# An encoder layer in float32: w_o by seven block products with the sums in DRAM, and every up-projection unit by seven products

## The chip, the cores and the metric

The kernel runs on one core of one Trainium2 chip. A core has TensorE (PE in the profile; matrix products into eight PSUM banks), VectorE (DVE), ScalarE (ACT), GpSimd (POOL) and SyncE (SP). Each takes its own instructions in order. DMAs are issued from the queues of SP, ACT and POOL. The metric is the device time of one execution in microseconds (us).

## The reference

One layer of a hybrid encoder on 512 tokens of width 2048, all in float32:

```python
h = rms_norm(x, pre_mix_g[l])
z = h @ w_in[l]                                  # q | k | v | u, 1024 columns each
a = chunked_attention(q, k, v, rel_bias[l])      # 8 heads of 128
p = multiscale_pool(u, pool_w[l], pool_scale[l])
m = jnp.concatenate([a, p], axis=-1) @ w_o[l]    # (512, 2048) @ (2048, 2048)
x = x + rms_norm(m, post_mix_g[l])
h = rms_norm(x, pre_ffn_g[l])
up = causal_dwconv(h @ w_up[l], conv_w[l], conv_b[l])   # 2 x 5632 columns, 3 taps
y = (gelu(up[..., :D_FF]) * up[..., D_FF:]) @ w_down[l] # (512, 5632) @ (5632, 2048)
x = x + rms_norm(y, post_ffn_g[l])
```

The gains, the relative bias, the pooling scale and the convolution's bias are random; the output is (1, 512, 2048).

## The kernel before, in words

Every large product is made three times on rounded parts. `split` (L127) writes a value's rounded part (`hi`, ScalarE, L129 or L132) and the rest (`lo`, VectorE, L130 or L133); `mm3` (L144) adds hi x hi, lo x hi and hi x lo into one PSUM bank. A tile that `mm3` reads therefore costs one ScalarE and one VectorE pass.

`Weights` (L55) hands out weight tiles of 128 x 1024 numbers (512 KB): `load_w` (L137) loads one on SP's queue into a raw tile (5 in the ring) and splits it into a ring of 8 (four pairs), four tiles ahead of use.

The stages follow each other on TensorE. Its order is the program's (L85); the instructions of the other engines and the DMA issues are put in order by a planner, which issues what is ready.

- **Projections.** h of the first norm stands with features on partitions (`hT`). q and k of head 0 are made while x arrives; then v of four heads, q and k per head, scores, softmax, values (L324, L349, L361), and eight projections u with pooling (`pool_keep`, L372). `mixT` holds the heads, `mT` the split concatenation.
- **w_o, features on partitions** (L464 to L528). 16 blocks of 128 output features; each is 16 x 3 matmuls whose stationary tile is w_o and whose moving tile is mT, 512 tokens wide. The result waits in `mg`, times the gain; squares are added up over features on POOL (L499).
- **The seam** (L531 to L599). Token sums by matmuls with ones (L160), a power on POOL for the reciprocal root mean square, 64 transposes that turn m back to tokens on partitions (L536) and store it in DRAM (`mtokd`), a spread of the token factors (L170), and `x2` (L568): multiply, add x, split into the second h (`gT`), square and add.
- **Up projection.** A unit u has 256 gate and 256 value columns. The first PLAIN = 3 units are whole products (L587 to L596, `up` L746). h goes in without the second norm's factor; the result is multiplied by it (`normed` L740, `keep_all` L917). The other 19 units, as 38 blocks k, use Strassen's scheme in Winograd's form: a block (128 x 2 columns, 512 tokens, 2048 features) is cut in two along all three, and seven products of half size (`seven` L928: 8 x 3 matmuls, 256 tokens wide) are combined afterwards (`keep_six` L902, `keep_all`). The weight sums for the products are made by adding DMAs from POOL into raw tiles (`add` L859) and one addition on VectorE (L866); the token factors, sums of quarters of h, are made once (`h_sums` L794). `Factors` (L822) orders the products and keeps four split ahead.
- **The rest of a unit.** Three taps (`taps` L708), gelu, product, and a store to DRAM (`gd`). `residual` (L934) makes x + norm(m) for the output rows beside blocks 4 to 20.
- **Down projection.** Five chunks of 1024 rows, also by seven products (`multiply` L681), summed in DRAM by adding DMAs (`keep_product` L688); the last two units plainly (`last`, L1127).

Memory is taken from pools that open and close; a tile in a pool that opens later waits for the tiles that lay there.

Of the kernel before, what the change touches and what calls it, by code (L numbers as in the profile page):

```python
# [30 lines left out]
PLAIN = 3  # L31
CU = 4
AHEAD = 3
SCALE = 1.0 / math.sqrt(DH)
# [41 lines left out]
def encoder_layer(ctx: ExitStack, tc: tile.TileContext, x, xT, vecs, rel, post_ffn,  # L76
# [15 lines left out]
    psum = ctx.enter_context(tc.tile_pool(name="psum", bufs=8, space=bass.MemoryType.PSUM))  # L92
    dram = ctx.enter_context(tc.tile_pool(name="dram", bufs=1, space=bass.MemoryType.DRAM))

    def bank(name):
        return psum.tile([P, 512], F32, tag="ps", name=name)
# [4 lines left out]
    def raw4(name):  # L101
        return big.tile([P, 1024], F32, tag="raw", bufs=5, name=name)
# [46 lines left out]
    def new_hT(name):  # L149

        return [[big.tile([P, 4, S], F32R, tag="hT", bufs=8, name=f"{name}{part}{i}") for i in range(4)]
                for part in "hl"]

    def blk(hT, kb, sl=slice(None)):
        return tuple(hT[part][kb // 4][:, kb % 4, sl] for part in range(2))
# [42 lines left out]
    for g in range(4):  # L198
        for j in range(2):
            specs += halves(f"u{2 * g + j}", w_in, head_cols("u", 2 * g + j), 8, P)  # L200
        if g:
            specs += pm_spec(g - 1)
    for n in range(8):
        s = halves(f"wo{n}", w_o, n * 256, 4, 256)
        specs += s[:-1] + pm_spec(3) + s[-1:] if n == 0 else s
    for u in range(PLAIN):
        gate, up_ = ([(f"w{p}{u}_{i}", w_up[u, p, :, i // 2, :, i % 2 * 512:(i % 2 + 1) * 512].rearrange(
            "m p c -> p m c"), 2, 512) for i in range(4)] for p in range(2))
        specs += [s for pair in zip(gate, up_) for s in pair] if u == 0 else gate + up_
# [4 lines left out]
    RR = const.tile([P, 2, S], F32, name="RR")  # L214
    R = RR[:, 0, :]
    rt = const.tile([P, NT], F32, name="rt")
    xt = [acc8(f"xT{i}", "AABB"[i]).rearrange("p (a b) -> p a b", a=4) for i in range(4)]
    hT = new_hT("hT")
# [21 lines left out]
    nc.sync.dma_start(vec[:, V_CONV:], vecs[:, V_CONV:])  # L240

# [6 lines left out]
    with tc.tile_pool(name="p1", bufs=2, reuse_waits="tile") as p1:  # L248
# [24 lines left out]
        zero = t512("u", bufs=2)[:, :P]  # L273
# [121 lines left out]
        def pool_mix(g, keep_):  # L395
            w = weights.get(f"pm{g}")
            d = [state.pop(("pool", g, a)) for a in range(2)]
            for j in range(2):
                ps = bank(f"pm{g}_{j}")
# [42 lines left out]
        mixT.append(acc8("mixT2", "B").rearrange("p (a b) -> p a b", a=4))  # L442
# [5 lines left out]
        u7 = project("u7")  # L448


        mT = new_hT("mT")

        def keep_mT(kb, ps, scale):
            split(*blk(mT, kb), ps, scale)

        for kb in range(4):
            split(*blk(mT, kb), mix(kb))
        pool_mix(2, keep_mT)
        for kb in range(4, 8):
            split(*blk(mT, kb), mix(kb))  # L460
        pool_keep(3, 1, u7)
        for kb in range(8, 12):
            split(*blk(mT, kb), mix(kb))
        wo0 = [bank(f"m{j}") for j in range(2)]  # L464

        def wo_block(ps, w, kb, j):
            mm3(ps, part(w, kb % 4, slice(j * P, (j + 1) * P)), blk(mT, kb), kb == 0, kb == KD - 1)

        for i in range(3):
            w = weights.get(f"wo0_{i}")  # L470
            for kb in range(4 * i, 4 * i + 4):
                for j in range(2):
                    wo_block(wo0[j], w, kb, j)
        pool_mix(3, keep_mT)
        w = weights.get("wo0_3")
        for kb in range(12, 16):
            for j in range(2):
                wo_block(wo0[j], w, kb, j)

    mg = [acc8(f"mg{i}", "AABB"[i]).rearrange("p (a b) -> p a b", a=4) for i in range(4)]  # L480
    rm = const.tile([P, NT], F32, name="rm")
    mtokd = [dram.tile([P, D], F32, name=f"mtokd{t}") for t in range(NT)]
    x2d = [dram.tile([P, D], F32, name=f"x2d{t}") for t in range(2, NT)]

    with tc.tile_pool(name="p2", bufs=2, reuse_waits="tile") as p2:
        ssum = p2.tile([P, S], F32, name="ssum", bufs=1)

        def wo_keep(cb, ps):
            sq = p2.tile([P, S], F32, tag="sq", bufs=2, name="sq")
            nc.scalar.activation(sq, ps, AF.Square)  # L490
            nc.scalar.activation(mg[cb // 4][:, cb % 4, :], ps, AF.Copy, scale=col(V_POSTMIX, cb))
            return sq

        sqs = []

        def wo_add(cb, ps):
            sqs.append(wo_keep(cb, ps))
            if cb:
                nc.gpsimd.tensor_add(ssum, sqs[-1], sqs[0] if cb == 1 else ssum)  # L499

        for j in range(2):
            wo_add(j, wo0[j])
        for n in range(1, 7):
            ps = [bank(f"m{2 * n + j}") for j in range(2)]
            for i in range(4):
                w = weights.get(f"wo{n}_{i}", 0 if n == 6 and i else None)
                for kb in range(4 * i, 4 * i + 4):
                    for j in range(2):
                        wo_block(ps[j], w, kb, j)
            for j in range(2):  # L510
                wo_add(2 * n + j, ps[j])
        xc = []

        def load_xc(kb):
            c = p2.tile([P, S], F32, tag="xc", bufs=5, name=f"xc{kb}")
            nc.scalar.dma_start(c, xT[kb * P:(kb + 1) * P, :])
            xc.append(c)

        ws = [weights.get(f"wo7_{i}", 3 - i) for i in range(4)]
        for kb in range(5):  # L520
            load_xc(kb)
        for j in range(2):
            ps = bank(f"m{14 + j}")
            for kb in range(KD):
                wo_block(ps, ws[kb // 4], kb, j)
            if j == 0:
                wo_add(14, ps)
        last = wo_keep(15, ps)  # L528
        weights.prefetch(2)

        mtok = [p2.tile([P, D], F32, name=f"mtok{t}", bufs=1) for t in range(NT)]  # L531

        def turn_back(t, g):
            ps = bank(f"mt{t}_{g}")
            for i in range(4):
                nc.tensor.transpose(ps[:, i * P:(i + 1) * P], mg[g][:, i, t * P:(t + 1) * P], ident)  # L536
            return t, g, ps

        def turned(t, g, ps, engine):
            dest = mtok[t][:, g * 512:(g + 1) * 512]  # L540
            if engine:
                nc.vector.tensor_copy(dest, ps)
            else:
                nc.scalar.activation(dest, ps, AF.Copy)
            nc.sync.dma_start(mtokd[t][:, g * 512:(g + 1) * 512], dest)

        psr = bank("Rm")
        token_sums(psr[:, NT:], ssum)
        before = p2.tile([P, NT], F32, name="before", bufs=1)
        nc.vector.tensor_scalar(before, psr[:, NT:2 * NT], 1.0 / D, EPS, op0=ALU.mult, op1=ALU.add)  # L550
        for t in range(2):
            turned(*turn_back(0, t), t)
        token_sums(psr, last)
        nc.vector.scalar_tensor_tensor(rm, psr[:, :NT], 1.0 / D, before, op0=ALU.mult, op1=ALU.add)
        nc.gpsimd.tensor_tensor(rm, rm, mhalf, op=ALU.pow)
        weights.prefetch(4)
        rest = [(0, 2)] + [(t, g) for t in range(1, 3) for g in range(3)]
        for i, (t, g) in enumerate(rest):
            turned(*turn_back(t, g), i % 2)
        spread(psr, rm)  # L560
        later = [(3, g) for g in range(3)] + [(t, 3) for t in range(NT)]
        pending = [turn_back(*p) for p in later[:3]]


        hT = new_hT("gT")
        ss2 = p2.tile([P, S], F32, name="ss2", bufs=1)

        def x2(kb):  # L568
            v = mg[kb // 4][:, kb % 4, :]
            nc.vector.tensor_mul(v, v, psr)  # L570
            (nc.gpsimd if kb % 2 else nc.vector).tensor_add(v, v, xc[kb])
            split(*blk(hT, kb), v, col(V_PREFFN, kb))
            sq = p2.tile([P, S], F32, tag="sq", bufs=2, name="sq2")
            nc.scalar.activation(sq, v, AF.Square)
            sqs.append(sq)
            if kb:
                nc.gpsimd.tensor_add(ss2, sq, sqs[-2] if kb == 1 else ss2)
# [22 lines left out]

    mixing.close()

# [154 lines left out]

# [460 lines left out]
```

## Time and profile before

| | |
|---|---|
| median of 3 runs | 1961.03 us (1959.75 to 1962.8) |
| profiled execution: its span, first to last instruction | 1954.2 us |
| what lies around the span, against the median | 6.8 us |
| TensorE busy | 1929.5 us |
| VectorE, ScalarE, POOL busy | 1405.5, 890.2, 311.7 us |
| w_o, first to last matmul | 405.6 to 582.5 us |
| seam, up to the first up-projection matmul | 582.5 to 591.9 us |
| plain units | 591.9 to 731.4 us |
| units by seven products | 731.4 to 1496.7 us |
| DMA | 335.51 MB, mean 172 GB/s |

The profile is of one execution. Each row of a group gives the line, the engine, the operation, what it writes and reads with shapes, the count, the busy time and the mean of one in ns, and the idle time before with what ended it. A matmul's listed length is longer than the distance between two, since they overlap.

### The profile page before, as it was taken

How to read it: one execution, taken by the hardware profiler on the slowest of the kernel's cores; microseconds unless marked ns; L12 is line 12 of the kernel's file. 1: busy time of each engine (PE TensorE's matmuls, PEld its weight loads, DVE VectorE, ACT ScalarE, POOL GpSimd, SP SyncE). 2: the span in 40 equal slices, each digit the busy share in tenths (PEclk: the TensorE clock that was granted, in tenths of full speed). 3: DMA queues.
4: the chain of work that ended last, by engine and by line, in shares of the span. 5: the costliest groups of instructions: out<-in, count | busy, mean ns of one | idle time of the engine just before them, and what ended most of it. 6: DMA issues, size and time to landing. Idle time of an engine off the chain costs nothing.

```text
span 1954.2 us, 28600 instructions
## 1 busy us (share of the span) xinstructions
PE 1929.5 (99%) x11594; PEld 1721.6 (88%) x11594; DVE 1405.5 (72%) x1573; ACT 890.2 (46%) x1092; POOL 311.7 (16%) x377
## 2 busy tenths in 40 slices
PE   9999999999999999999999999999999899999998
PEld 7888888888887889999999999999998688888886
DVE  5554255562229867787888878788888999998877
ACT  6333233242236434444454445444445555465443
POOL 4000000001117001111111211111110121221221
PEclk9999999999999999999999999999999999999999
DMA  7433332332235356768887887767675789999997
GB/s 241 116 89 92 92 92 70 98 127 96 97 97 198 119 160 152 163 161 220 214 212 198 201 225 183 188 150 184 167 183 179 264 213 263 246 222 231 214 223 228
DMA packets 176499, 335.51 MB, mean 172 GB/s; under 512 B 10480, under 2 KB 78448, under 8 KB 175088
## 3 DMA queue, kind: packets, MB, share of 16 engines
q1 hardware_dynamic: 135824, 219.39, 33.6%
q0 software_dynamic: 38240, 110.12, 29.9%
q10 hardware_dynamic: 2304, 4.20, 0.7%
q8 instruction: 90, 1.47, 0.3%
q14 instruction: 41, 0.34, 0.0%
HBM read 272.84 MB, written 60.82 MB: 171 GB/s over the span
## 4 chain that ended last, share of the span: by engine, by line
PE 92%; DVE 4%; DMA 2%; issue 1%; ACT 0%; SPq 0%; POOL 0%; ACTq 0%; POOLq 0%; DVEq 0%
PE q L146 15%; PE q L147 14%; PE q L145 14%; PE p L145 6%; PE p L147 6%; PE p L146 6%; PE m L147 3%; PE m L145 3%; PE m L146 3%; PE up L146 2%; PE up L147 2%; PE up L145 2%; PE u L145 1%; PE u L146 1%; PE v L146 1%; PE v L145 1%
## 5 line engine op out<-in xcount | busy, mean ns | idle before, releaser
L146 PE MATMUL q<-gTl,wfh 128*128 128x256 f32 x1216 | 344.0, 283 | 0.0
L147 PE MATMUL q<-gTh,wfl 128*128 128x256 f32 x1216 | 343.9, 283 | 0.0
L145 PE MATMUL q<-gTh,wfh 128*128 128x256 f32 x1216 | 343.8, 283 | 0.0
L145 PEld LDWEIGHTS q<-gTh,wfh 128*128 128x128 f32 x1216 | 233.1, 192 | 0.0
L147 PEld LDWEIGHTS q<-gTh,wfl 128*128 128x128 f32 x1216 | 233.1, 192 | 0.0
L146 PEld LDWEIGHTS q<-gTl,wfh 128*128 128x128 f32 x1216 | 232.9, 192 | 0.0
L146 PE MATMUL p<-bl,ah 128*128 128x512 f32 x560 | 221.2, 395 | 4.7 <-DVE bl L130 4.7
L145 PE MATMUL p<-bh,ah 128*128 128x512 f32 x560 | 222.4, 397 | 2.8 <-ACT ah L129 2.8
L147 PE MATMUL p<-bh,al 128*128 128x512 f32 x560 | 221.8, 396 | 2.3 <-DVE al L130 2.3
L129 ACT ACTIVATE wfh<-wx 128x1024 fp32r<-128x1024 f32 x152 | 158.8, 1056 | 120.5 <-PE q L146 80.3
L130 DVE TENSOR_TENSOR wfl<-wx,wfh 128x1024 fp32r<-128x1024 f32 x152 | 183.9, 1220 | 35.6 <-ACT wfh L129 35.5
L130 DVE TENSOR_TENSOR bl<-b,bh 128x2048 fp32r<-128x2048 f32 x70 | 159.2, 2285 | 14.2 <-PE p L146 8.4
L129 ACT ACTIVATE bh<-b 128x2048 fp32r<-128x2048 f32 x70 | 133.0, 1913 | 68.7 <-DVE b L660 52.6
L146 PEld LDWEIGHTS p<-bl,ah 128*128 128x128 f32 x560 | 105.7, 189 | 30.1 <-DVE bl L130 5.4
L129 ACT ACTIVATE wfh<-wy 128x1024 fp32r<-128x1024 f32 x76 | 80.6, 1060 | 113.3 <-PE q L146 72.7
L147 PEld LDWEIGHTS p<-bh,al 128*128 128x128 f32 x560 | 105.9, 189 | 29.0 <-DVE al L130 3.7
L145 PEld LDWEIGHTS p<-bh,ah 128*128 128x128 f32 x560 | 105.7, 189 | 27.8 <-ACT ah L129 3.7
L860 POOL DMA_DIRECT2D wx<-in_w_up x76 | 67.5, 889 | 381.8 <-DVE wfl L130 366.3
L702 POOL DMA_DIRECT2D sum<-part x60 | 72.5, 1235 | 256.1 <-DVE part L693 120.3
L130 DVE TENSOR_TENSOR wfl<-wy,wfh 128x1024 fp32r<-128x1024 f32 x76 | 92.7, 1220 | 26.8 <-ACT wfh L129 26.3
L146 PE MATMUL q<-h4l,wfh 128*128 128x256 f32 x304 | 86.0, 283 | 0.0
L146 PE MATMUL q<-h7l,wfh 128*128 128x256 f32 x304 | 86.0, 283 | 0.0
(430 smaller groups left out, 4844.3 us busy)
## 6 DMA issues: line engine op xcount, KB each, us to landing
b<-in_w_down SPq DMA_DIRECT2D x42, 1024.0 KB, 7.8
wx<-in_w_up POOLq DMA_DIRECT2D x76, 512.0 KB, 6.7
sum<-part POOLq DMA_DIRECT2D x70, 512.0 KB, 7.8
wx<-in_w_up SPq DMA_DIRECT2D x40, 512.0 KB, 5.7
wy<-in_w_up SPq DMA_DIRECT2D x38, 512.0 KB, 5.4
wz<-in_w_up SPq DMA_DIRECT2D x38, 512.0 KB, 6.1
wy<-in_w_up POOLq DMA_DIRECT2D x38, 512.0 KB, 7.1
gd<-ca POOLq DMA_DIRECT2D x40, 256.0 KB, 3.3
```

Of the source, the lines that this page charges most:

```text
L129: rounded = nc.scalar.activation(hi, src, AF.Copy)
L130: nc.vector.tensor_sub(lo, src, f32(hi))
L145: nc.tensor.matmul(ps, l[0], r[0], start=first, stop=False)
L146: nc.tensor.matmul(ps, l[0], r[1], start=False, stop=False)
L147: nc.tensor.matmul(ps, l[1], r[0], start=False, stop=last)
L702: nc.gpsimd.dma_start(dest, v, accum_op=ALU.add)
L860: nc.gpsimd.dma_start(self.raw[k, what], self.block(k, m, kh), accum_op=ALU.add)
```

## The change

w_o is computed by the same seven-product scheme, now with tokens on partitions: the stationary tile is a 128-token piece of a factor made from the mixed heads, the moving tile is 512 columns of a factor made from w_o. Four of the seven w_o factors are sums of quarters of w_o; they are formed in DRAM (`wo_sum`) by plain copies on SP's queue and adding DMAs on POOL's, 32 steps of 1 MB, one of which is written before each projection (`next(summing)`) and before every second tile of v. Each product of 1024 x 256 tokens x 1024 columns takes 4 bank groups (`wo_product`); `mixed` adds the products up on VectorE, takes squares along the row on ScalarE and multiplies by the gain.

With tokens on partitions the norm is a factor per partition: `norms` makes x + norm(m), stores it, takes the second norm and scales; `turned` transposes the normed x (64 transposes) and writes it with the second gain as h. Tokens 0 to 255 are done during the last two products, tokens 256 to 511 after them.

The up projection takes this normed h, so the multiplication by the spread factor disappears. All 22 units (44 blocks) go by seven products. For the first EARLY = 4 blocks the products that need only tokens 0 to 255 (1 and 2) come first, with the transposes of the other tokens between them; then the other five for blocks 0 and 1, then for 2 and 3, with all their weight sums by adding DMAs. The token factors are combined from h in between (`combine`). Signs of the odd columns are taken into the convolution weights. PSUM banks are named by hand. The residual step, `mtokd`, the token sums and the spread are gone.

```diff
-PLAIN = 3
+EARLY = 4
@@
-        return big.tile([P, 1024], F32, tag="raw", bufs=5, name=name)
+        return big.tile([P, 1024], F32, tag="raw", bufs=6, name=name)
@@
+    WO_ORDER = 1, 2, 6, 7, 4, 5, 3
+    for n in WO_ORDER:
+        for cc in range(2):
+            s = [(f"wo{n}{cc}_{q}", rows(wo_factor[n], q * 256, cc * S, 2, S), 2, S) for q in range(4)]
...
+    def wo_sums():
...
+        steps = [(5, wo_quarter(1, 1), 0), (7, wo_quarter(0, 0), 0), (5, wo_quarter(1, 0), 1), (7, wo_quarter(1, 0), 1),
+                 (6, wo_sum[5], 0), (6, wo_quarter(0, 0), 1), (3, wo_sum[6], 0), (3, wo_quarter(0, 1), 1)]
+        for n, src, add in steps:
+            for r in range(4):
+                if add:
+                    nc.gpsimd.dma_start(piece(wo_sum[n], r), piece(src, r), accum_op=ALU.add)
+                else:
+                    nc.sync.dma_start(piece(wo_sum[n], r), piece(src, r))
+                yield
@@
         def project(name, between=None):
             ps = bank(name)
+            next(summing, None)
@@
             for c in range(8):
+                if c % 2 == 0:
+                    next(summing, None)
                 w = weights.get(f"v{i}_{c}")
@@
+        def wo_product(i, cc, ps, between=None):
+            for q in range(4):
+                w = weights.get(f"wo{i}{cc}_{q}")
...
                 for j in range(2):
+                    kb = 2 * q + j
+                    for t in range(2):
+                        l = first_factor(kb, t) if i == 1 else at(wo_f[i], kb, slice(t * P, (t + 1) * P))
+                        mm3(ps[t], l, part(w, j), kb == 0, kb == 7)
@@
+            self.order = [(k, i) for k in range(EARLY) for i in (1, 2)]
+            for k in range(0, EARLY, 2):
+                self.order += [(j, i) for i in (5, 7, 6, 4, 3) for j in (k, k + 1)]
@@
+        def norms(t, xs):
+
+            r = rms[0][t]
+            rstd2(r, ssq[:, 2 * t:2 * t + 2, :])
+            for c in range(2):
+                cs = slice(c * C, (c + 1) * C)
+                for j in range(2):
+                    v = m[2 * t + j]
+                    nc.vector.scalar_tensor_tensor(v[:, cs], v[:, cs], r[:, j:j + 1], xs[j][:, cs],
+                                                   op0=ALU.mult, op1=ALU.add)
+                    nc.scalar.activation(xs[j][:, cs], v[:, cs], AF.Square,
+                                         accum_out=ssq2[:, 2 * t + j, c:c + 1])
+            r = rms[1][t]
+            rstd2(r, ssq2[:, 2 * t:2 * t + 2, :])
...
+                    nc.scalar.activation(xn[j][:, cs], m[2 * t + j][:, cs], AF.Copy, scale=r[:, j:j + 1])
             for j in range(2):
+                nc.sync.dma_start(x2d[j] if t else out[j * P:(j + 1) * P, :], m[2 * t + j])
@@
+        xn = norms(1, xs)
+        turning = turned(1, xn, 0)
+        for k, i in factors.order[:2 * EARLY]:
             seven(k, i)
+            for _ in range({(2, 1): 2, (2, 2): 3, (3, 1): 3}.get((k, i), 0)):
+                h1 = next(turning)
...
+        combine(5, lambda b11, b12, b21, b22: minus(b11, b12, b11))
+        combine(7, lambda b11, b12, b21, b22: minus(b22, b12, b12))
+        combine(6, lambda b11, b12, b21, b22: minus_sum(b11, b22, b11))
+        combine(4, lambda b11, b12, b21, b22: minus_sum(b11, b21, b21))
+        combine(3, lambda b11, b12, b21, b22: b22)
@@
         nc.vector.tensor_add(z[:, T:3 * T], done_bank(k, "34"), z[:, T:3 * T])
-            nc.vector.tensor_mul(z, z, flat(RR))
```

More of the change, by code (lines that the diff above doesn't have):

```diff
@@ L448, in encoder_layer @@
         u7 = project("u7")
[L451 to L460, printed above, removed]
-        pool_keep(3, 1, u7)
[L462 to L467, printed above, removed]
@@ L482, in encoder_layer @@
[L482 to L577, printed above, removed]
-            if kb + 5 < KD:
-                load_xc(kb + 5)
-        for kb in range(2):
-            x2(kb)
-        for p in pending:
-            turned(*p, 0)
-        for p in later[3:]:
-            turned(*turn_back(*p), 0)
-        ups = [[bank(f"up0_{p}_{j}") for j in range(2)] for p in range(2)]
-        for kb in range(KD):
-            if kb % 4 == 0:
-                w = [weights.get(f"w{p}0_{kb // 4}") for p in range(2)]
-            if kb + 2 < KD:
-                x2(kb + 2)
-            for p in range(2):
-                for j in range(2):
-                    mm3(ups[p][j], part(w[p], j, slice(kb % 4 * P, (kb % 4 + 1) * P)), blk(hT, kb),
-                        kb == 0, kb == KD - 1)
-        psr = bank("R2")
-        token_sums(psr, ss2)
-        rstd(rt, psr[:, :NT])
@@ L601, in encoder_layer, with eight, put, mf @@
-    mixing.close()
+        pool_keep(3, 1, u7)
+        for _ in summing:
+            pass
+        def eight(name):
+            v = hT4(name, 8)
+            return [v[:, :, :4, :], v[:, :, 4:, :]]
+        wo_f = {i: eight(f"mf{i}") for i in (2, 6, 5, 3)}
+        def put(f, k0, n, v):
+            hi, lo = (f[k0 // 4][:, half, k0 % 4:k0 % 4 + n, :] for half in range(2))
+            split(hi, lo, v)
+        def mf(i, k0, n, v):
+            put(wo_f[i], k0, n, v)
+        def at(f, kb, sl=slice(None)):
+            return tuple(f[kb // 4][:, half, kb % 4, sl] for half in range(2))
@@ new lines, in seven @@
+    def seven(k, i):
+        w = factors.get()
+        ps, half = half_bank(k, i)
+        for kb in range(8):
+            mm3(ps[:, half], part(w, kb), at(h_f[i], kb), kb == 0, kb == 7)
+    m = [None] * NT
+    for i, tag in ((7, "raw1"), (4, "wh")):
+        wo_f[i] = hold_factor(tag, f"mf{i}")
+    pp, gain = hold_rows("wl", "pp")
+    nc.sync.dma_start(gain, post_mix[None, :].to_broadcast([P, D]))
+    for group in GROUPS:
+        mf(7, *group, quarter(0, 1, *group))
+    for group in GROUPS:
+        mf(4, *group, quarter(1, 0, *group))
@@ new lines, in keep_all, with first_left, load, parts @@
+    def keep_all(k):
+        z = zs.pop(k)
+        nc.vector.tensor_add(z[:, T:3 * T], done_bank(k, "34"), z[:, T:3 * T])
+        z = z.rearrange("p (a b) -> p a b", a=2)
+        u = k // 2
+        if k % 2:
+            product(u, gates.pop(u), z)
+        else:
+            gates[u] = gate(u, z)
+    def first_left():
+        def load(i, j):
+            v = raw4(f"a{i}{j}").rearrange("p (u n) -> p u n", u=CU)
+            nc.sync.dma_start(v, gd[0][i][:, :, j, :])
+            return v
+        def parts(v):
+            hi, lo = (w4(f"a{p}").rearrange("p (u n) -> p u n", u=CU) for p in "hl")
+            split(hi, lo, v)
+            return hi, lo
+        for j in range(2):
+            yield parts(load(0, j))
@@ new lines, in encoder_layer, with next_first @@
+    rights, lefts, firsts = [right(0, cc) for cc in range(2)], first_left(), []
+    for r in rights:
+        next(r)
+    end = factors.last
+    def next_first():
+        _, i = ORDER0[len(firsts)]
+        r = rights[0].send(i)
+        firsts.append((i, next(lefts), r))
+    for k, i in factors.order[2 * EARLY:]:
+        seven(k, i)
+        if (k, i) == (end - 1, 3):
+            next_first()
+        if i == 6:
+            keep_six(k)
+            if k == end:
+                next_first()
+        if i == 3:
+            keep_all(k)
@@ L990, in encoder_layer @@
+    cycle[:] = spare
+    firsts = [(i, multiply(l, r)) for i, l, r in firsts]
     phase.close()
```

579 lines of the change are left out of this document (325 added, 254 removed).

## The prediction

> **What bounds the kernel now.** I read the page first, then the matmul groups by stretch, then TensorE's timeline at the seams, then its waits.
>
> ```profile
> span 1954.2 us, 28600 instructions
> ...
> PE 1929.5 (99%) x11594; PEld 1721.6 (88%) x11594; DVE 1405.5 (72%) x1573; ACT 890.2 (46%) x1092; POOL 311.7 (16%) x377
> ...
> PE 92%; DVE 4%; DMA 2%; issue 1%; ACT 0%; SPq 0%; POOL 0%; ACTq 0%; POOLq 0%; DVEq 0%
> ```
>
> TensorE is busy for 99% of the span and carries 92% of the chain that ended last. So an edit is worth the matmul time that it removes, less every new wait of TensorE. A matmul's listed duration is no price, since matmuls overlap; the price is the distance from one start to the next. The next two fences give it: the matmuls of each stage, counted by stretch (columns: stretch, length, TensorE busy with count, clock, DMA share, GB/s), and TensorE's timeline at the seams (start, length, instruction, count, wait).
>
> ```profile
> 404.00:590.00 186.00, 174.43 (x768) 1.00 0.34 110
> 590.00:732.00 142.00, 134.96 (x576) 0.99 0.49 155
> 731.00:1497.00 766.00, 765.49 (x6384) 1.00 0.75 189
> ```
>
> ```profile
> 405.57 0.39 PE L145 MATMUL m<-mTh,wo_0h 128*128 128x512 f32 x1
> ...
> 582.47 0.95 PE L163 MATMUL Rm<-ones,ssum 128*128 128x1 f32 x8
> ...
> 585.00 3.25 PE L536 MATMUL mt<-ident,mg 128*128 128x128 f32 x28
> 588.09 0.60 PE L173 MATMUL Rm<-ident,rm 128*128 128x128 f32 x4
> ...
> 591.89 0.49 PE L145 MATMUL up<-gTh,w_0h 128*128 128x512 f32 x1
> ...
> 611.23 0.50 PE L146 MATMUL up<-gTl,w_1h 128*128 128x512 f32 x1 [2.65 <-DVE gTl L133]
> ...
> 731.35 0.28 PE L145 MATMUL q<-gTh,wfh 128*128 128x256 f32 x1
> ...
> 1496.68 0.39 PE L145 MATMUL p<-bh,ah 128*128 128x512 f32 x1
> ```
>
> From 405.57 to 582.47 stand the 768 matmuls of w_o and 12 of the last pool map: 176.90/780 = 0.2268 us for 512 columns. From 731.35 to 1496.68 stand 6384 of 256 columns: 765.33/6384 = 0.1199 us. Half the columns cost 53%, so seven products of half size (7/8 of the columns) gain, but less than 1/8.
>
> **The change, part by part: TensorE's own work.**
>
> 1. w_o. Seven products, each 2 column halves x 4 tiles x 2 blocks x 2 token blocks x 3 = 96 matmuls of 512 columns, make 672 instead of 768. 96 x 0.2268 = 21.8 us less.
> 2. Three plain units of the up projection (576 matmuls of 512) become six more blocks of 168 matmuls of 256: 576 x 0.2268 = 130.6 against 1008 x 0.1199 = 120.9. 9.7 us less.
> 3. The seam from 582.47 to 591.89 is 9.42 us. Its 64 transposes are replaced by 64 of the normed x, at (588.09 - 585.00)/28 = 0.110 us, so 7.1 us stay; token sums and spreads go. 2.3 us less.
> 4. The plain units took 731.35 - 591.89 = 139.46 us, 8.9 more than their 130.6: waits for the split of h (2.65 of it above), the slow matmuls after them, the second token sums. All of that goes. 8.9 us less.
>
> Together 42.7 us less: 1954.2 becomes 1911.5 us of span before any new wait. The multiplication by the spread rms in every block goes too (38 on VectorE), as do the residual loads; neither is on TensorE's path, so I cost them at nothing.
>
> **New waits: the sums in DRAM.** 16 plain copies of 1 MB on SP's queue and 16 adding DMAs of 1 MB on POOL's are written between the projections, one step each. Who issues them when? The planner orders every queue but TensorE's by readiness.
>
> ```profile
> 2.27 0.10 POOL L375 MEMSET u<- 128x16 f32 x1
> ```
> ```profile
> 424.90 0.86 ACTq L516 DMA_DIRECT2D xc<-in_xT  x2
> ```
>
> The first clears a tile of the pooling, which is written in the code after seven heads, and runs at 2.27 us. The second is a load written at the seventh w_o group (near 560 us), issued at 424.90, as soon as its memory was free. The first eight copies need no memory and wait for nothing, so I expect them on SP's queue as soon as it has a gap, ahead of v's later tiles and not spread over 300 us.
>
> ```profile
> 22.46 0.37 SPq L140 DMA_DIRECT2D v_4r<-in_w_in  x1
> ...
> 29.68 0.37 SPq L140 DMA_DIRECT2D v_6r<-in_w_in  x1
> ```
> ```profile
> 29.26 0.39 PE L145 MATMUL v<-v_0h,hTh 128*128 128x512 f32 x1
> ```
> ```profile
> 48.60 1.04 ACT L129 ACTIVATE v_6h<-v_6r 128x1024 fp32r<-128x1024 f32 x1
> ```
> ```profile
> q1 hardware_dynamic: 135824, 219.39, 33.6%
> q0 software_dynamic: 38240, 110.12, 29.9%
> ```
> ```profile
> v_6r<-in_w_in SPq DMA_DIRECT2D x2, 512.0 KB, 3.9
> ```
>
> v_6 is issued at 29.68; TensorE needs it at 29.26 + 6 x 24 x 0.2268 = 61.9, less some 2.3 us for its split, so 59.6. The cushion from issue is 29.9 us, of which the load itself takes 3.9 (median to landing, the row above). Plain DMAs run at 219.39 MB / (0.336 x 1954.2 us) = 334 GB/s, adding and other POOL DMAs at 110.12 / (0.299 x 1954.2) = 188 GB/s. Eight copies (8.4 MB) take 25.1 us, which just uses the cushion up; four adding DMAs that start as the first copies land (4.2 MB) take 22.3 us of the same engines. Bounds 0 and 22 us; I take 10, the middle, since no row shows a copy from DRAM to DRAM and how the two queues share is not shown. The rest of the chain of sums has the length of the projections; a weight tile there is used up in 24 x 0.2268 = 5.4 us and six raw tiles are ahead, some 33 us of cover.
>
> The Trainium skill bears on this (DMA: Bandwidth & Descriptors, "Issuing engines are not separate DMA queues"): DMAs started by different engines run on the same 16 DMA engines and interleave, so putting half of the sums on POOL's queue shields no load. The rows above fit it without proving it; taken strictly it gives the upper bound of 22 us in place of 10.
>
> **New waits: w_o and the seam behind it.** The prices are these, for VectorE, ScalarE, POOL and DMA.
>
> ```profile
> L130 DVE TENSOR_TENSOR wfl<-wx,wfh 128x1024 fp32r<-128x1024 f32 x152 | 183.9, 1220 | 35.6 <-ACT wfh L129 35.5
> ...
> L693 DVE TENSOR_TENSOR part<-p,part 128x512 f32<-128x512 f32 x60 | 39.7, 684 | 7.7 <-PE p L147 7.6
> ...
> L939 DVE SCALAR_TENSOR_TENSOR xr<-mr,rm,xr 128x1024 f32<-128x1024 f32 x8 | 10.3, 1285 | 33.4 <-DMA mr<-mtokd 33.4
> ```
> ```profile
> L129 ACT ACTIVATE wfh<-wx 128x1024 fp32r<-128x1024 f32 x152 | 158.8, 1056 | 120.5 <-PE q L146 80.3
> ```
> ```profile
> L555 POOL TENSOR_TENSOR rm<-rm,mhalf 128x4 f32<-128x4 f32 x1 | 1.0, 1032 | 11.6 <-DVE rm L554 11.6
> ```
> ```profile
> wx<-in_w_up POOLq DMA_DIRECT2D x76, 512.0 KB, 6.7
> ...
> wx<-in_w_up SPq DMA_DIRECT2D x40, 512.0 KB, 5.7
> ```
>
> - Start of w_o. A weight tile now feeds 12 matmuls (2.7 us), not 24, as in the up stage (24 x 0.1199 = 2.9 us). VectorE's work in w_o: 56 weight splits x 1.22 = 68, six token factors of two splits each 15, their sums 7, some 44 operations of 512 columns x 0.68 = 30, norm and pool tail 11: 131 of 152 us, covered by four tiles split ahead (10.9 us). Most of it falls in the first two products. 1 us, bounds 0 and 5.
> - Norm of tokens 256 to 511, after the last w_o product: adds and gains 4 x 0.68 = 2.7, row sum and power 1.5 (1.03 of it POOL), four multiply-adds 5.1, the last square 1.1, power 1.5, two scaled copies 2.1, then the first transpose: 14.0 us, and with three or four weight splits between them on VectorE 18.3. Cover: five early products of 24 matmuls, 14.4 us. 5 us with the hand-overs, bounds 0 and 9. Late next is the transposed h, and behind it the combinations.
> - Combinations for the factors 5, 7, 6, 4, 3: four of two sums and two splits, one of two splits, 18 x 1.22 = 22.0 on VectorE; with ten weight splits (12.2) and the sums of two blocks (about 4) 38 us, against ten products of 2.9 = 28.8 on TensorE. Short by 9; four weights split ahead give back 4.9. 4 us, bounds 0 and 9.
> - The third and fourth block's first raw tile lies in memory that the combinations free. Freed about 23 us after TensorE enters the first of the ten products; then 5.7 load, 6.7 adding DMA, 2.3 split: 37 us, against 28.8 + 4. 3 us, bounds 0 and 9.
>
> Sum of new waits 10 + 1 + 5 + 4 + 3 = 23 us, bounds 0 and 54. 1911.5 + 23 = 1934.5 us of span. The median of the runs, 1961.03, lies 6.8 us above the profiled 1954.2; with that the forecast is **1941 us**.
>
> **The rivals.**
>
> - *All new waits are hidden.* For it: TensorE is idle for 24.7 us in all now (1954.2 less 1929.5), and in the up stage VectorE is busy for 83 of 100 us without a wait (the row below). Against it: the norm behind the last product is a chain. 1911.5 + 6.8 = 1918; with a few microseconds left 1920.
>
> ```profile
> 900.00:1000.00 100.00, 100.00 (x836) 100.00 (x835) 83.44 (x99) 49.12 (x59) 17.69 (x21) 1.00 0.81 206
> ```
> - *VectorE bounds w_o.* For it: 131 of 152 us, bunched at the start. It would lose some 15 us there beyond the above: 1956, no change that can be told.
> - *The sums hold the queues: slower.* SP and POOL take their instructions in order. A copy that waits for an adding DMA holds SP's weight loads behind it, and one that waits for a copy holds POOL's clearing of the masked scores, for which VectorE waits. The 16 adding DMAs take 16.8 MB / 188 GB/s = 89 us; if the projections wait for that beyond the cover of 33 us, 56 us are lost. 1911.5 + 13 + 56 + 6.8 = 1987. For it: the hoisted load and clearing above. Against it: DMA is busy only 31% of the second 100 us, as the row below shows, and the planner puts the waiting copies later too. It decides from the point where the sums cost over 30 us.
>
> ```profile
> 100.00:200.00 100.00, 100.00 (x487) 84.71 (x486) 53.04 (x109) 36.62 (x73) 2.32 (x16) 1.00 0.31 90
> ```
>
> The Trainium skill's page on DMA (same section as above) speaks for this rival, since nothing separates the two queues' transfers.
>
> **How the numbers follow.** Forecast 60% (its own range 1922 to 1960), all hidden 15%, VectorE bounds w_o 5%, queues held 20%. 0.2% of the time is 3.9 us, about what a measurement of this kernel can tell from no change. Faster than 1957: nearly all of the first two cases and a little of the third, 72%. Within: 8%. Slower than 1965: the last case, 20%. The range takes in the first case's lower end and most of the last: 1916 to 1986.
>
> **What would show each step.** 672 matmuls of 512 columns for w_o at 0.227 and 7392 of 256 at 0.120 show parts 1 and 2. The sums show in SP's timeline: copies bunched before 40 us, or spread; and in TensorE's waits for v's splits between 45 and 90 us. The seam shows as waits of transposes for ScalarE's scaled copies and of the fifth to tenth product for VectorE. The forecast is wrong if TensorE waits over 40 us in the first 200 us, or if the sum of its waits there is near zero, or if the spacing of matmuls changes.

## The result, and the profile after

The changed kernel takes **2010.57 us** (median of four runs, 2008.93 to 2012.22) against 1960.39 us before (1958.04 to 1962.8): a ratio of 1.0258, 95% interval 1.0242 to 1.0273. It is slower by 50 us, where the forecast was 20 us faster, and lies 25 us beyond the range's upper end. The profiled execution has a span of 2007.1 us, 52.9 more than before. One run of the last kernel below, at 2933.31 us with a granted clock of 0.589 against 0.99 in its others, is left out of that kernel's median.

The page of the changed kernel: the span, busy times, two rows of the forty slices (50 us each), and the chain that ended last by engine.

```profile
span 2007.1 us, 29439 instructions
...
PE 1892.6 (94%) x11898; PEld 1720.3 (86%) x11898; DVE 1414.0 (70%) x1616; ACT 948.5 (47%) x1178; POOL 288.7 (14%) x381
...
PE   9509999999999899999999999999999899999997
...
DMA  9999333224677877676767676767676689999997
...
PE 85%; DMA 5%; DVE 4%; issue 3%; ACT 1%; SPq 1%; POOL 0%; POOLq 0%; DVEq 0%; ACTq 0%
```

TensorE's busy time fell by 36.9 us (1929.5 to 1892.6), as intended. But its second and third slices read 5 and 0: TensorE works for half of the time from 50 to 100 us and not at all from 100 to 150, while the DMA engines are busy in the first four slices. One wait explains that. TensorE's waits (what waited and for whom: total us, times, longest):

```profile
PE R L178 <- POOL rt L173: 75.0, 1, 75.0
PE q L153 <- DVE wfl L136: 8.4, 2, 5.4
...
PE xt L893 <- ACT xn L880: 3.9, 2, 3.2
```

L178 spreads the reciprocal rms of the first norm, L173 is the power on POOL that makes it, a tile of 128x4. The power takes 1.4 us; why did it come 75 us late? The chain that ended last, cut to that stretch (start, us, what):

```profile
73.54 0.80 PE R L168 x8
74.74 13.20 SPq L231
...
89.31 38.39 DMA wo_sum<-wo_sum
...
128.20 16.34 DMA wo_sum<-in_w_o
144.56 7.84 DMA wo_sum<-wo_sum
...
152.90 0.88 POOL wo_sum L229
153.78 1.09 POOL rt L173
154.91 1.12 PE R L178 x4
```

From the token sums (73.54) to the spread (154.91) the chain runs through sums in DRAM: L231 is a plain copy, L229 an adding DMA. POOL's timeline (start, us, instruction, idle time ahead of it and what ended it) shows how they got ahead of the power:

```profile
34.04 1.14 POOL L229 DMA_DIRECT2D wo_sum<-in_w_o  x1
...
65.85 0.89 POOL L229 DMA_DIRECT2D wo_sum<-in_w_o  x1 [13.69 <-DMA wo_sum<-in_w_o]
...
128.20 0.88 POOL L229 DMA_DIRECT2D wo_sum<-in_w_o  x1 [22.57 <-DMA wo_sum<-wo_sum]
...
152.90 0.88 POOL L229 DMA_DIRECT2D wo_sum<-in_w_o  x1 [11.38 <-DMA wo_sum<-wo_sum]
153.48 1.38 POOL L173 TENSOR_TENSOR rt<-rt,mhalf 128x4 f32<-128x4 f32 x1
...
177.05 0.88 POOL L229 DMA_DIRECT2D wo_sum<-in_w_o  x1 [2.16 <-DMA wo_sum<-wo_sum]
177.61 0.48 POOL L367 MEMSET s<- 64x64 f32 x1
```

Fourteen of the 16 adding DMAs stand on POOL's queue ahead of the power (thirteen, by a miscount, in the first expectation below) and the other two ahead of the first score mask (L367), though the code writes them one by one between the projections. From the fourth on POOL mostly stands idle until a transfer in DRAM has landed, and takes nothing else meanwhile. SP's queue looks the same; its columns are the start, how long the issue or the group of issues holds the queue, and the instruction.

```profile
74.74 13.20 SPq L231 DMA_DIRECT2D wo_sum<-in_w_o  x1
...
102.60 42.43 SPq L231 DMA_DIRECT2D wo_sum<-wo_sum  x3
145.13 0.52 SPq L146 DMA_DIRECT2D q_0r<-in_w_in  x1
152.20 0.47 SPq L231 DMA_DIRECT2D wo_sum<-wo_sum  x1
152.78 0.52 SPq L352 DMA_DIRECT2D bias<-in_rel  x1
```

Copies of unfinished sums hold a weight load until 145 us, and the first load of the score bias goes out at 152.78. The issue at 74.74 is another matter: that copy reads only w_o and waits for no sum, yet its issue holds the queue for 13.20 us; a run below comes back to this. Behind the stall the schedule is the old one, later: w_o starts at 483.00 us against 405.57 before, 77.43 later. The excess is all made there; what follows is shorter than before by 77.43 - 52.9 = 24.5 us.

Last, the stretches of 25 us (as in the prediction: length, then busy time of PE, PEld, DVE, ACT and POOL, clock, DMA share, GB/s):

```profile
75.00:100.00 25.00, 4.93 (x22) 3.74 (x20) 0.67 (x1) 0.00 (x0) 1.76 (x2) 0.67 1.06 284
100.00:125.00 25.00, 0.00 (x0) 0.00 (x0) 0.00 (x0) 0.00 (x0) 1.76 (x2) 0.50 1.05 236
125.00:150.00 25.00, 0.00 (x0) 0.00 (x0) 0.00 (x0) 0.00 (x0) 3.52 (x4) 0.50 1.03 273
```

From 100 to 150 us no engine computes (POOL's busy time is its DMA issues), and the DMA engines are fully busy. So three readings compete. **T**: the in-order queue of POOL, held by adding DMAs. **S**: the in-order queue of SP, held by copies. **B**: the 32 MB themselves, so early, starve the core, whoever issues them.

### The profile page after: what moved, and what is told of

It reads as the page before. It is cut to its first block, busy times and chain, and to the rows that moved or that the text cites. A ratio compares the mean times of both kernels' runs of the same rounds, so it can differ in the third digit from the quotient of the medians.

```text
span 2007.1 us, 29439 instructions
## 1 busy us (share of the span) xinstructions
PE 1892.6 (94%) x11898; PEld 1720.3 (86%) x11898; DVE 1414.0 (70%) x1616; ACT 948.5 (47%) x1178; POOL 288.7 (14%) x381
## 4 chain that ended last, share of the span: by engine, by line
PE 85%; DMA 5%; DVE 4%; issue 3%; ACT 1%; SPq 1%; POOL 0%; POOLq 0%; DVEq 0%; ACTq 0%
PE q L152 15%; PE q L153 15%; PE q L151 15%; PE p L152 6%; PE p L153 6%; PE p L151 6%; DMA wo_sum<-wo_sum 2%; PE m L152 2%; PE m L151 2%; PE m L153 2%; PE u L152 1%; PE v L152 1%; PE u L153 1%; PE v L151 1%; PE u L151 1%
## 5 line engine op out<-in xcount | busy, mean ns | idle before, releaser
L151 PE MATMUL q<-gT,wfh 128*128 128x256 f32 x1408 | 399.1, 283 | 0.0
L152 PE MATMUL q<-gT,wfh 128*128 128x256 f32 x1408 | 398.8, 283 | 0.0
L153 PE MATMUL q<-gT,wfl 128*128 128x256 f32 x1408 | 398.7, 283 | 0.0
L153 PE MATMUL q<-h,wfl 128*128 128x256 f32 x1056 | 301.0, 285 | 8.4 <-DVE wfl L136 8.4
L151 PE MATMUL q<-h,wfh 128*128 128x256 f32 x1056 | 300.9, 285 | 0.1
L152 PE MATMUL q<-h,wfh 128*128 128x256 f32 x1056 | 300.7, 285 | 0.0
L135 ACT ACTIVATE wfh<-wx 128x1024 fp32r<-128x1024 f32 x172 | 182.1, 1059 | 198.2 <-PE q L152 138.4
L152 PEld LDWEIGHTS q<-gT,wfh 128*128 128x128 f32 x1408 | 270.6, 192 | 0.2 <-DVE gT L136 0.2
L151 PEld LDWEIGHTS q<-gT,wfh 128*128 128x128 f32 x1408 | 270.6, 192 | 0.0
L153 PEld LDWEIGHTS q<-gT,wfl 128*128 128x128 f32 x1408 | 270.6, 192 | 0.0
L136 DVE TENSOR_TENSOR wfl<-wx,wfh 128x1024 fp32r<-128x1024 f32 x172 | 210.0, 1222 | 78.2 <-ACT wfh L135 78.1
L153 PEld LDWEIGHTS q<-h,wfl 128*128 128x128 f32 x1056 | 204.7, 194 | 8.8 <-DVE wfl L136 8.8
L151 PEld LDWEIGHTS q<-h,wfh 128*128 128x128 f32 x1056 | 204.7, 194 | 0.4 <-issue 0.3
L152 PEld LDWEIGHTS q<-h,wfh 128*128 128x128 f32 x1056 | 204.7, 194 | 0.0
L136 DVE TENSOR_TENSOR bl<-b,bh 128x2048 fp32r<-128x2048 f32 x70 | 159.3, 2287 | 13.4 <-PE p L152 6.8
## 6 DMA issues: line engine op xcount, KB each, us to landing
wo_sum<-in_w_o POOLq DMA_DIRECT2D x16, 1024.0 KB, 16.8
```

Of the source, the lines that this page charges most:

```text
L135: rounded = nc.scalar.activation(hi, src, AF.Copy)
L136: nc.vector.tensor_sub(lo, src, f32(hi))
L151: nc.tensor.matmul(ps, l[0], r[0], start=first, stop=False)
L152: nc.tensor.matmul(ps, l[0], r[1], start=False, stop=False)
L153: nc.tensor.matmul(ps, l[1], r[0], start=False, stop=last)
```

## The experiments

Each kernel ran beside the kernel before, whose median lay between 1959.65 and 1961.19 us; so a difference of 1 or 2 us between two of the experiments says nothing.

### The same sums in the kernel before

```
+    wo_sum, wo_sums() as in the change; next(summing, None) at the same places
     (w_o itself as before: the sums are not read)
```

> The kernel before with nothing but the 16 copies and 16 adding DMAs written at the same places; their results are not read. T: the power of the first norm stands behind 15 of the adding DMAs here, so TensorE waits for rt some 75 to 90 us, and the time is 1961 + 75 to 90 = 2036 to 2050. B: about 35 to 60 us more by late loads, with waits of TensorE for weights. S: as B, with the waits for q and k weights after 100 us. If the stall comes from the new w_o or up projection and not from the sums: no change, 1961.

Measured: 2043.03 us (one run; before 1959.65), within T's range. TensorE's waits in it:

```profile
PE R L173 <- POOL rt L168: 80.4, 1, 80.4
```

The 32 transfers alone make the stall, with the same victim. Neither the new w_o nor the new up projection has a part in it.

### No sums at all

```
-    wo_factor = {1: ..., 2: ..., 4: ..., **wo_sum}
+    wo_factor = {1: ..., 2: ..., 4: ..., 5: quarter, 7: quarter, 6: quarter, 3: quarter}
-    summing = wo_sums()
+    summing = iter(())
```

> The 16 copies and 16 adding DMAs in DRAM are left out; the products 5, 7, 6 and 3 of w_o read plain quarters of w_o instead of sums, so the outputs are not the reference's; every instruction on the engines stays. T, B and S all expect the 75 us wait to go. It gives the floor without any cost of the sums: 2010.6 - 77.5 (w_o starts 77.43 us later than before, 483.00 against 405.57) = 1933. If the sums cost more than the stall in the first 200 us (bandwidth in w_o, late loads there), it comes out under 1930; if the prediction's other terms hold it is 1934.5 - 10 + 3.5 = 1928.

Measured: 1934.32 us, ratio 0.9868 (0.9853 to 0.9883). This is the floor, and it lies within 2 us of the 1933 that the shift of w_o's start gives. So within that margin all that the sums cost is the stall.

### The adding DMAs behind the power

```
+    with tc.issue_after(power of the first norm):
         nc.gpsimd.dma_start(piece(wo_sum[n], r), piece(src, r), accum_op=ALU.add)
```

> One order is added: each of the 16 adding DMAs stands on POOL's queue behind the power that makes the reciprocal rms of the first norm; copies and all else stay. Theory T (POOL takes its queue in order, and the power stood behind 13 adding DMAs that wait for their copies): the 75.0 us wait of TensorE for rt goes; the power runs near 75 us as before, and the time falls by about 77 to some 1933 us; if the adding DMAs now hold the masks of the scores for a while, up to 1950. Rival B (the 32 MB of transfers themselves starve TensorE, whoever issues them): the transfers are the same and as early, so the stall only moves to late weight loads and the time stays over 1985. Rival S (SP's queue is held by copies that wait for adding DMAs, so weight loads come late): the copies stay where they were, TensorE then waits for q and k weights between 90 and 200 us, and the time stays over 1970.

Measured: 2001.03 us, ratio 1.0199 (1.0178 to 1.0221). The expectation of T, 1933 to 1950, failed. The power runs at 73.66 us, and the wait for it is gone, but another stands in its place. Waits of TensorE, then VectorE's timeline, in this kernel:

```profile
PE pt L388 <- DVE s L377: 61.3, 6, 56.3
```
```profile
165.00 0.62 DVE L368 SCALAR_TENSOR_TENSOR s<-s,bias 128x128 f32<-128x128 f32 x2 [46.68 <-DMA bias<-in_rel]
195.58 0.29 DVE L372 TENSOR_REDUCE nm<-s 128x1 f32<-128x128 f32 x1 [29.96 <-POOL s L370]
```

The second head's scores wait 46.68 us for their bias, whose load stands on SP's queue behind the copies, and then 29.96 us for a mask, which stands on POOL's queue behind the adding DMAs. Taking one victim out of the queue only presents the next one. The time also lies in the ranges of B and S, but the late weights that both expected do not show among TensorE's waits. From here on S is no longer a rival of T but a partner, with the score bias as its victim.

### The power elsewhere, and then POOL empty of victims

```
-    rstd(rt, psr[:, :NT])
+    nc.vector.tensor_scalar(rt, psr[:, :NT], 1.0 / D, EPS, op0=ALU.mult, op1=ALU.add)
+    nc.scalar.activation(rt, rt, AF.Sqrt)
+    nc.vector.reciprocal(rt, rt)
```

> The changed kernel with the power of the first norm made by a square root on ScalarE and a reciprocal on VectorE; sums, copies and queues stay. All 16 adding DMAs then stand ahead of the first score mask on POOL. T: TensorE no longer waits for rt, but the masks cannot run before 175 us, so VectorE's scores and then TensorE's transposes of the probabilities wait some 60 to 75 us: the time is 1990 to 2010, hardly better. If the power itself was the only victim: 1934 to 1940.

Measured: 2014.03 us (one run), 4 us above T's range. The second kernel adds this to it:

```
-    nc.gpsimd.memset(s[:CHUNK, n - CHUNK:n], -1e30)
+    nc.vector.memset(s[:CHUNK, n - CHUNK:n], -1e30)
```

> As the run with the power made elsewhere, and the score masks are cleared by VectorE too, so that POOL holds nothing that the projections or the scores wait for. Copies and adding DMAs stay as the changed kernel has them, and so does SP's queue, where the first load of the score bias stands behind 15 of the 16 copies. S (SP's queue alone is enough): the bias load is issued near 152 us and lands near 175, VectorE stands at the first scores, and the time stays at 2000 to 2015. T alone (POOL's queue was needed for the stall): no stall, 1934 to 1945.

Measured: 2008.1 us (one run), as S expected. VectorE's timeline in the first and in the second:

```profile
175.54 0.29 DVE L365 SCALAR_TENSOR_TENSOR s<-s,bias 128x128 f32<-128x128 f32 x1 [89.47 <-DMA bias<-in_rel]
```
```profile
174.07 0.29 DVE L365 SCALAR_TENSOR_TENSOR s<-s,bias 128x128 f32<-128x128 f32 x1 [81.22 <-DMA bias<-in_rel]
```

T named the masks as the next victim; in both it is the score bias on SP's queue, issued at 150.90 and 152.44 us, and VectorE, which also takes its work in order, then keeps back the split of a weight for which TensorE waits (67.1 and 62.2 us). In the first kernel the masks would have been little better: POOL clears the first at 179.00 us. In the second kernel POOL holds nothing that is needed, and the time is about the same. So SP's hold alone is enough. In the changed kernel the power on POOL stands first in TensorE's way, and the bias behind it; both queues are paced by the same chain of sums, so either hold lasts about as long.

### Orders on both queues, and on one

```
+    anchor["POOL"] = the last power or score mask written
+    anchor["SP"] = the last weight load written
+    with tc.issue_after(anchor["POOL"]):   # around each adding DMA
+    with tc.issue_after(anchor["SP"]):     # around each copy
```

> Each adding DMA stands on POOL's queue behind the last power or score mask written before it, and each copy on SP's queue behind the last weight load written before it; all else stays. T: the sums then run beside the projections, no instruction of POOL or SP waits long behind one of them, and the time is that without sums, about 1930 to 1936: faster than both kernels. B: the same 32 MB spread over 380 us cost little, so it too expects under 1945; S the same. T differs from B and S by this being equal to the first run here (orders on POOL alone) within some 5 us, or better than it by no more than what the masks wait there.

Measured: **1934.58 us**, ratio 0.9868 (0.9851 to 0.9884). With the same 32 transfers the time is that without any (1934.32). T expected it to equal the run with an order behind the power alone, or to gain what the masks wait there; it beats that run by 66 us, the masks and the bias.

> Of the two orders of the paced kernel only the one on POOL is kept: each adding DMA behind the last power or score mask written before it; the copies on SP's queue go where the planner puts them. T (waiting adding DMAs ahead of POOL's small work are the whole cause): no stall, 1934 to 1940. S (copies that wait on SP hold the weight loads and need an order of their own): TensorE waits for weights between 100 and 300 us, over 1950.

> Only the order on SP is kept: each copy behind the last weight load written before it; the adding DMAs go where the planner puts them, seven of them still ahead of the power of the first norm. T in its plain form (any adding DMA ahead of the power stalls it): TensorE waits for rt tens of us, over 1960. Convoy (the stall grows because the two queues wait for each other in turn, an adding DMA for a copy that stands behind a load on SP that waits for what POOL holds): with the copies out of the way only the seventh adding DMA matters, whose copy lands near 74 us, so the power is a few us late at most and the time is 1934 to 1945.

Measured: with the order on POOL alone 1935.61 us, ratio 0.9873 (0.9853 to 0.9892); with the order on SP alone 1961.01 us, ratio 1.0001 (0.9987 to 1.0014). The first is enough: once the adding DMAs are late, the planner puts the copies that need them late too. In the second TensorE waits for the power again:

```profile
PE R L180 <- POOL rt L175: 25.3, 1, 25.3
```

There POOL held its seventh adding DMA until 102.77 us for a copy that I expected near 74: SP's queue came to that copy at 80.61 us only, and its issue took 13.62 us. An adding DMA ahead of the power is a risk even when the copies are in their place. It cost some 26 us here and not 76: with the copies tied, only seven adding DMAs stand ahead of the power instead of fourteen.

### Bytes: half of them, and all of them without waits

```
-            return src[r * 256:(r + 1) * 256, :]
+            return src[r * 256:r * 256 + 128, :]        # with plain quarters in w_o
```

> The 32 transfers of the changed kernel stay in number, order and waits, but each moves 512 KB instead of 1 MB (the lower half of each piece is left out); the products read plain quarters of w_o, so the outputs are not the reference's. On POOL's queue 14 adding DMAs stand ahead of the power of the first norm. Bytes (the queue decides who waits, the saturated DMA engines decide how long: DMA share 1.03 to 1.06 between 75 and 150 us): the chain from 20 to 153 us halves to end near 90 us, the wait for rt falls from 75 to 10 to 20 us, time 1943 to 1955. Latency (each link of the chain of copies and adding DMAs takes a fixed time whatever its size): the wait stays over 50 us, time over 1985.

Measured: 1960.72 us, ratio 1.0003 (0.9993 to 1.0013). TensorE's wait for rt and a stretch of this kernel:

```profile
PE R L178 <- POOL rt L173: 25.1, 1, 25.1
```
```profile
75.00:100.00 25.00, 4.75 (x21) 3.57 (x19) 0.48 (x1) 0.00 (x0) 3.25 (x4) 0.63 1.03 262
```

Same number of transfers, same order, half the bytes: the wait falls from 75.0 to 25.1 us. Both ranges were missed, that of bytes by 5 us and that of a fixed time by 25. The power runs at 103.48 instead of 153.48, and counted from the first copy near 20 us the chain shrinks from 133 to 83 us, not quite to the half. The weight loads of that stretch share the DMA engines, which stay at a share of 1.03; that this is the whole remainder is not shown. So the queues decide **who** waits, and the bytes on full DMA engines mostly decide **how long**. A fixed time for each link, whatever its size, is out as the main part.

```
-    nc.gpsimd.dma_start(piece(wo_sum[n], r), piece(src, r), accum_op=ALU.add)
+    nc.gpsimd.dma_start(free.pop()[:, :], a piece of w_o)      # 32 scratch pieces, no one reads them
-    nc.sync.dma_start(piece(wo_sum[n], r), piece(src, r))
+    nc.sync.dma_start(free.pop()[:, :], a piece of w_o)
```

> The products read plain quarters of w_o (outputs are not the reference's), and 32 DMAs of 1 MB, 16 on SP's queue and 16 on POOL's, each go to a scratch of their own that nobody reads; none waits for another, so all are issued early. T and convoy: no instruction of POOL waits, the power runs at 75 us, TensorE's wait for rt is zero; time 1934 to 1945, the rest being loads that share the DMA engines. B (bytes early starve TensorE): the same bytes, earlier still, so TensorE waits 40 us or more for weights and the time is over 1970.

Measured: 1981.61 us, ratio 1.0107 (1.0087 to 1.0128). The figure of T and the convoy was wrong, B's right. TensorE's timeline and a stretch show where:

```profile
17.39 0.80 PE L151 MATMUL q<-hT,q_0h 128*128 128x512 f32 x1 [5.66 <-ACT q_0h L135]
...
35.82 0.79 PE L151 MATMUL q<-hT,q_0h 128*128 128x512 f32 x1 [5.49 <-ACT q_0h L135]
...
149.80 0.79 PE L153 MATMUL q<-hT,q_1l 128*128 128x512 f32 x1 [12.52 <-DVE q_1l L136]
```
```profile
25.00:50.00 25.00, 13.89 (x29) 8.26 (x30) 5.93 (x9) 5.90 (x10) 0.00 (x0) 0.57 0.99 337
```

With no sum to wait for, POOL's transfers went out from 1.40 us on, eleven of them before 20 us, among the first loads of x and weights. TensorE waits for the first weights, and the token sums come at 106.09 us against 73.09 in the run without sums. So bytes that are early enough cost by themselves, 33 us here.

The 12.52 us at 149.80 have another cause. VectorE's and SP's timelines:

```profile
148.33 0.29 DVE L368 SCALAR_TENSOR_TENSOR s<-s,bias 128x128 f32<-128x128 f32 x1 [29.05 <-DMA bias<-in_rel]
148.53 1.22 DVE L136 TENSOR_TENSOR q_1l<-q_1r,q_1h 128x1024 fp32r<-128x1024 f32 x1
```
```profile
74.39 17.89 SPq L234 DMA_DIRECT2D free<-in_w_o  x1
...
138.16 0.52 SPq L355 DMA_DIRECT2D bias<-in_rel  x1
```

VectorE waits for the score bias, whose load leaves SP's queue at 138.16 us, behind copies, and the split of the weight stands behind the scores. This is S again, without a copy that waits for a sum: the issue of a single copy holds the queue for 17.89 us, with the DMA engines at a share of 1.01 to 1.02. So where they were full, copies held a queue even though they depended on no other transfer; what an issue spends that time on was not tried.

The early loss is not the stall of the changed kernel, where v ended in time (73.38 us against 72.78 before) and TensorE waited for no weight there for more than 0.7 us. The run shows that taking the waits out of the way is no cure without moving the bytes.

### The waits behind w_o

Two edits on the kernel with both orders. The first puts four differences on POOL:

```
-            nc.vector.tensor_sub(out, a, b)
+            nc.gpsimd.tensor_sub(out, a, b)
```

> The paced kernel with the four plain differences of the seven-product factors of h (128x1024 each) on POOL instead of VectorE. The prediction's term for the combinations (VectorE has 38 us of work against 28.8 us of products) expects the wait of the first products of the combined h (5.45 + 2.99 + 1.15 us in the paced kernel) to shrink by up to 4 x 1.2 = 4.9 us, so 1930 to 1934. If the chain through ScalarE's rounding sets that wait and not VectorE's load, or POOL is slower than 1.2 us by more than it frees: same or up to 6 us slower, 1935 to 1941.

Measured: 1939.76 us, ratio 0.9898 (0.9881 to 0.9914), 4 to 5 us more than without it, the second case of the expectation. One wait of 7.6 us for the split of a combined factor appears, and less of the wait for weights goes away:

```profile
PE q L154 <- DVE gT L136: 7.6, 1, 7.6
...
PE q L155 <- DVE wfl L136: 3.7, 2, 3.0
```

The second writes four products between the combinations:

```
     combine(5, ...); combine(7, ...)
+    for k, i in factors.order[2 * EARLY:2 * EARLY + 2]: seven(k, i)
     combine(6, ...)
+    for k, i in factors.order[2 * EARLY + 2:2 * EARLY + 4]: seven(k, i)
     combine(4, ...); combine(3, ...)
```

> The paced kernel with the first four products of the combined h written between the combinations (5 and 7, two products, 6, two products, 4 and 3) instead of behind all of them, so that the splits of their weights on VectorE come ahead of the later combinations. If the order of VectorE's work sets the wait of 5.45 us ahead of the first product of the combined h (the split that it waits for runs behind nine operations of factors 6 and 4): that wait shrinks by 3 to 5 us and the slow matmuls behind it too, 1927 to 1932. If VectorE's load sets it: the wait moves to a later product, 1933 to 1937.

Measured: **1931.3 us** (median of three runs, 1930.69 to 1931.59), ratio 0.9852 (0.9833 to 0.9872); the span is 1929.5 against 1933.4 with the orders alone. It beats both kernels, and is the lowest time here, though the intervals of this and the kernel with the orders alone overlap. Its waits:

```profile
PE q L153 <- DVE z L1008: 7.3, 1, 7.3
...
PE xt L897 <- ACT xn L884: 3.7, 2, 3.1
```

The wait for weight splits (9.6 us in three waits) is gone; one of 7.3 us for the sum that frees a bank of PSUM came in its place. So the time is that of the first case, while the wait moved as in the second: the order of VectorE's work set part of it. That the rest is VectorE's load is not shown.

## Why the prediction was wrong, point by point

The kernel with both orders lets the other terms be read without the stall. Its waits, its stages on TensorE's timeline, and one stretch:

```profile
PE q L155 <- DVE wfl L136: 9.6, 3, 5.4
...
PE xt L897 <- ACT xn L884: 4.3, 2, 3.6
```
```profile
405.67 0.39 PE L153 MATMUL mx<-wo_0h,s 128*128 128x512 f32 x1
...
564.99 0.36 PE L153 MATMUL q<-gT,wfh 128*128 128x256 f32 x1
...
615.33 0.58 PE L155 MATMUL q<-h,wfl 128*128 128x256 f32 x1 [5.45 <-DVE wfl L136]
...
1475.31 0.39 PE L153 MATMUL p<-bh,ah 128*128 128x512 f32 x1
```

- **TensorE's own work: right.** From the start of w_o to the first p the kernel before took 1496.68 - 405.57 = 1091.1 us; less the 42.7 of the four parts that is 1048.4. Here it is 1475.31 - 405.67 = 1069.6, so 21.2 us of waits and what follows them, most of which the next point accounts for. w_o itself, with 684 matmuls at 0.2268 and half of the transposes, should last 155.1 + 3.5 = 158.6 us, and lasts 564.99 - 405.67 = 159.3 with the other small things in it; so the rival that VectorE bounds w_o did not show.
- **New waits behind w_o: right in kind, 13 us forecast, 21.2 measured.** The start of w_o costs under 1 us (1 forecast), the norm of the later tokens 4.3 (5), the combinations and raw tiles 9.6 (4 + 3). The size that was off: matmuls after a wait are slow, which had no term. After the 5.45 us wait 28 matmuls ran 0.213 us apart instead of 0.120, 2.6 us lost; the transposes and products behind the waits for `xn` lost some 1.6 us in the same way. The last 2 us or so are not traced to a row.
- **Sums in DRAM: the step that failed.** It saw the hoisting, and priced it as weights that come late for v: 10 us, bounds 0 and 22. v lost 0.6 us, and what the term left out, the holds on the two queues, moved the start of w_o by 77.43 us. The sentence that broke is "The rest of the chain of sums has the length of the projections": it holds for where the code writes the sums, but the rows that were quoted for the hoisting hold for every step, also for those that wait. All 32 went into the first 177 us.
- **The rival "the sums hold the queues" was the right mechanism at 20% and 1987 us.** It failed in place and in size. In place: the first victim on POOL is the power of the first norm, for which TensorE already waits at 154.91 - 75.0 = 79.9 us, 6 us behind the token sums, then the masks; on SP it is the score bias. In size: it gave the chain a cover of 33 us, from raw weight tiles. There is no such cover, since the victims are not weights; 89 us of adding DMAs less 33 were 56, and the whole stall came to 75.0 plus the slow restart. The range ended at 1986, 1 us under this rival's own price. The argument against it, that the planner puts waiting copies late too, did not hold: 15 of the 16 copies went out ahead of the first bias load. Nor did the DMA share of 0.31 in the second 100 us, for the sums themselves filled it (1.05 and 1.03 above). Why the planner took them so early was not tried; it may reckon with shorter transfers than full DMA engines give.
- **The forecast's own test worked**: "wrong if TensorE waits over 40 us in the first 200 us"; it waits 75.
- **The 6.8 us beside the span** were no constant: the medians lie 3.5 us above the span in the changed kernel, 1.2 with the orders. Wherever a run's time stands beside its own span, the two are 1.7 to 2.1 us apart; the rest of the 6.8 is the difference between the profiled execution and the median one.

In the prediction's terms, 1911.5 + 13 + 8.2 more behind w_o, and 0.7 elsewhere (0.1 ahead of w_o, 0.6 from the first p on), give the 1933.4 us span of the kernel with the orders. From there to the changed kernel's 2007.1 are 73.7 us: 77.3 by which w_o starts later, from where the sums stand on the queues, less 3.6 behind that, which are not traced.

The prediction cited the Trainium skill (DMA: Bandwidth & Descriptors, "Issuing engines are not separate DMA queues"). Its rule held: in the run without waits transfers issued on POOL's queue delay SP's first loads, with a DMA share of 0.99. What decided this case stands on another page of the Trainium skill (PSUM — Partial Sum Buffer, "Engine vs sequencer instructions"): the queues of ScalarE, VectorE and GpSimd are strictly first in, first out. The power behind the waiting DMAs (153.48 us) agrees with it, and so does VectorE's weight split behind the scores (81.22 us).

## What to carry to other kernels

Before a DMA that must wait for another is put on a queue, list what else that queue carries and who stands for it within the next microseconds: a 1.4 us operation of a small tile cost 75 us, and taking it away only showed the next one. The place in the code did not say when the planner issued a transfer; if one needs no memory, tie it by an order to work of the same queue that is due at the time you mean. Price a chain of DRAM sums by bytes on full DMA engines, against the cover of the most urgent thing behind it on each queue; on full DMA engines count the issue too, which held SP's queue for up to 17.89 us here.

## What was not expected of the hardware

- A copy or an adding DMA of 1 MB within DRAM has no one price: from issue to landing 21.3 us (the eight copies out of w_o) and 16.8 us (adding) at the median in the changed kernel, where the DMA engines are full, 8.5 and 11.5 us when they are spread by the orders.
- The granted clock reads 0.50 while TensorE stands, and the restart is slow: after the 75 us wait 512-column matmuls run 0.43 us apart for some 3 us, against 0.2268, and after a wait of only 5.45 us 256-column ones run 0.213 apart for 5.9 us, against 0.120. The Trainium skill (TensorE: Matmul & The Clock Gate, "What's actually happening") gives half rate after an idle window and full rate after some 3.4 us of activity; the ratios, 1.9 and 1.8, come near it; the second stretch is longer than that figure.
- Work moved from VectorE to a nearly idle POOL made the kernel 4 to 5 us slower, so the idle share of an engine was no measure of what a move would gain.
